# The last norm and the store of a two-block model: from feature-major to token-major output

## The chip, the cores and the metric

The kernel runs on one core of a Trainium2 chip. The metric is the device time of one execution in microseconds (us). Before the change the median of three runs is 906.7 us (905.62, 906.70 and 907.33). One execution was profiled; all rows below are from it.

## The reference, cut to what matters

Two transformer blocks follow each other on 256 tokens of width 1024. The change concerns the very end of the second: the down projection of its MLP, the residual, and the final norm, which divides each token by the root of the mean square over its 1024 features and scales each feature by `g_final`.

```
def rms_norm_2(x, g, eps=1e-5):
    xf = x.astype(float32)
    y = xf * rsqrt(mean(xf * xf, axis=-1, keepdims=True) + eps)
    return y * g
...
    u = rms_norm_2(x, g_mlp) @ w_up          # 256x1024 @ 1024x4096
    x = x + square(relu(u)) @ w_down         # 256x4096 @ 4096x1024
return rms_norm_2(x, g_final)                # 256x1024, float32
```

## The kernel before, in words

**Layout.** Activations are feature-major: a tile has 128 partitions, each a feature, and the 256 tokens (S) lie along the free axis. The width of 1024 is KC = 8 such slices, so xT, the residual stream, is [128, 8, 256]. A sum over features is therefore a sum over partitions and slices, and PE (TensorE) does it with a matmul against the constant tile ones, which holds 1/1024 everywhere: its result has the mean in every one of the 128 partitions.

**Weights.** Class Stream brings a weight tile of 128x1024 by DMA (fetch, line 134, on SyncE's queue, SP), ACT (ScalarE) rounds it to a high part (line 152) and DVE (VectorE) or POOL (GpSimd) subtracts to get the low part (line 158). Function mm3 (lines 358 to 360) then does three matmuls per product: high by high, high by low, low by high.

**Order.** PE's instructions keep the order in which the program writes them; on the other engines and queues a scheduler orders what is ready, and in the part that is looked at here it also keeps the written order.

**The end of the program** (from line 1682). For each of the 8 output slices j, function down does 4 weight tiles of 8 products (96 matmuls) into a PSUM bank. Function residual (line 436, DVE) adds it to xT. Class SumSq squares the slice and adds it up: POOL squares (line 310) and accumulates into ss_acc (line 316) for slices 0 to 6, ACT squares slice 7 into ss_last (line 308). ACT also scales the slice by g_final into og[:, 0, j] (line 1691). The mean needs two matmuls: ones by ss_acc (line 320, put inside the last down, after its second weight tile) and ones by ss_last (line 323, the last thing PE does). Function rsqrt takes Ln and Exp on ACT (line 253), half of that on ACT (line 269), and one Newton step on DVE (lines 271, 272 and 274), all on 128x256. Then line 1696 multiplies og by this row, in three pieces: slices 0 and 1 on DVE, 2 to 4 on DVE, 5 to 7 on POOL, and line 1697 stores each piece, the first and the third by SP, the second by ACT's queue. The host turns the result to token-major. The tile pool tmp, of which rsqrt and SumSq take their tiles, stands in SBUF ahead of the weight buffers (wraw, whi, wlo) and of all pools that are opened later.

Of the kernel before, what the change touches and what calls it, by code (L numbers as in the profile page):

```python
# [8 lines left out]
F32 = mybir.dt.float32  # L9
# [4 lines left out]
ALU = mybir.AluOpType  # L14
# [4 lines left out]
P = 128  # L19
S = 256  # L20
D = 1024
KC = D // P
# [90 lines left out]
class Stream:  # L113
# [53 lines left out]
    def next(self):  # L167
        if not self.ready:
            self.load()
        return self.ready.pop(0)  # L170
# [3 lines left out]
def tile_kernel(ctx: ExitStack, tc: tile.TileContext, a, out: bass.AP):  # L174
    nc = tc.nc
    ctx.enter_context(tc.manual_schedule(engines={mybir.EngineType.PE}))
    V, A, G, PE = nc.vector, nc.scalar, nc.gpsimd, nc.tensor
# [13 lines left out]
    def bank(pool=None, name="bank"):  # L191
        pool = pool or ps_sm
        return pool.tile([P, 512], F32, tag="b", name=name)

    def mmbank():
        return bank(ps_mm, "mmb")
# [19 lines left out]
    def pv(name, j=0, w=1):  # L216
        return par[:, PC[name] + j : PC[name] + j + w]

    def cgv(name):
        return cg[:, CG[name][0] : CG[name][1]]  # L220

    ident = cgv("ident")
# [22 lines left out]
    def lookup(name, *args, **kw):  # L245


        if table["set"] != name:
            load = A.preload_act_table_set(name).ins
            for u in table["users"]:  # L250
                tc.add_manual_dep(load, u.name, NOSYNC, reason="table set")
            table.update(set=name, load=load, users=[])
        ins = A.activation(*args, **kw).ins  # L253
        tc.add_manual_dep(ins, table["load"].name, NOSYNC, reason="table set")
        table["users"].append(ins)
        return ins
# [4 lines left out]
    def rsqrt(mean, eps, n=S, name="rs", pool=None):  # L261

        pool = pool or tmp
        l = tmp.tile([P, n], F32, tag="rs_l", name="rs_l", bufs=1)
        y = tmp.tile([P, n], F32, tag="rs_y", name="rs_y", bufs=1)
        lookup(LNEXP, l, mean, AF.Ln, bias=EPS[eps])
        lookup(LNEXP, y, l, AF.Exp, scale=-0.5)
        yh = l
        A.mul(yh, y, -0.5)
        t = tmp.tile([P, n], F32, tag="rs_t", name="rs_t", bufs=1)  # L270
        V.scalar_tensor_tensor(t, mean, float(eps), y, op0=ALU.add, op1=ALU.mult)
        V.tensor_tensor(t, t, y, op=ALU.mult)
        r = pool.tile([P, n], F32, tag=name, name=name, bufs=2 if name == "rs" else 1)
        V.scalar_tensor_tensor(r, t, -3.0, yh, op0=ALU.add, op1=ALU.mult)
        return r
# [79 lines left out]
    def mm3(dst, hi, lo, x, k, first, last):  # L355

        xh, xl = x[:, k, 0, :], x[:, k, 1, :]
        PE.matmul(dst, lhsT=hi, rhs=xh, start=first, stop=False, skip_group_check=True)  # L358
        PE.matmul(dst, lhsT=hi, rhs=xl, start=False, stop=False, skip_group_check=True)  # L359
        PE.matmul(dst, lhsT=lo, rhs=xh, start=False, stop=last, skip_group_check=True)  # L360

    def g_wide(st, x, b):

        done = 0
        while done < KC:
            k0, nk, hi, lo = st.next()
            for k in range(nk):
                mm3(b[:, :S], hi[:, k, :], lo[:, k, :], x, k0 + k, k0 + k == 0, k0 + k == KC - 1)
                yield
            done = k0 + nk  # L370

    def settle(st, b, n=6):


        if not st.ready:
            st.load()
        hi = st.ready[0][2]
        for _ in range(n):
            PE.matmul(b[:, :S], lhsT=hi[:, 0, :], rhs=hi[:, 0:2, :].rearrange("p k c -> p (k c)"), start=True, stop=True)

    def run(gen):
        for _ in gen:
            pass

    def run_pair(*gens, late=2):

        for g in gens:
            for _ in range(KC - late):
                next(g)
        for g in gens:  # L390
            run(g)

    def down(st, n, x):

        b = mmbank()
        for _ in range(n):
            k0, nk, hi, lo = st.next()
            for k in range(k0, k0 + nk):
                mm3(b[:, :S], hi[:, k - k0, :], lo[:, k - k0, :], x, k, k == 0, k == x.shape[1] - 1)
            yield  # L400
        yield b[:, :S]
# [31 lines left out]
    def residual(j, ps, scale, gain, xnew, ss, mark=None):  # L433

        xj = xT[:, j, :]
        ins = V.scalar_tensor_tensor(xj, ps, float(scale), xj, op0=ALU.mult, op1=ALU.add).ins  # L436
        if mark:
            behind(ins, mark)
        parts = split(xnew, j, xj, gain) if xnew is not None else None
        for s, g in ss:  # L440
            s.add(xj, g)
        return parts
# [37 lines left out]
    ss = SumSq(fast=True)  # L480
# [11 lines left out]
    def hidden(pool, chunks):  # L492

        t = pool.tile([P, chunks * 2 * S + HOME], F32R, name="h")
        return t[:, HOME:].rearrange("p (k i t) -> p k i t", k=chunks, i=2)
# [153 lines left out]
    ss0, ss = ss, SumSq(split=True)  # L649
# [4 lines left out]
    with ExitStack() as rs_ctx:  # L654
# [209 lines left out]
        rstd = rsqrt(ss.mean(), 1e-6)  # L864
# [121 lines left out]
        for t in range(2, 16):  # L986
# [5 lines left out]
                op=ALU.mult,  # L992
# [22 lines left out]
        def columns(tl, w, i):  # L1015

            return n8(tl).rearrange("p n (b i t) -> p n b i t", i=2, t=w)[:, :, :, i, :]

        def per_head(tl):
            return lambda h, n: n8(tl)[own[h], n]  # L1020

        def products(lhsT, rhs):
            b = bank()
            for n in range(8):
                for h, o in enumerate(own):
                    PE.matmul(n8(b)[o, n], lhsT=lhsT(h, n), rhs=n8(rhs)[o, n], start=True, stop=True, skip_group_check=True)  # L1026
                if n % FILL[9] == FILL[9] - 1:
                    fill(FILL[10])
            return b
# [26 lines left out]
        for i, q in enumerate(halves):  # L1056
            b = products(per_head(Y16[i]), T[:, q])
            A.copy(columns(P1[i], 16, 0), columns(b, 16, 0))

        for i, q in enumerate(halves):  # L1060
            b = bank()
# [7 lines left out]
        for i, q in enumerate(halves):  # L1069
            bT = products(per_head(G_[:, q]), P1[i])  # L1070
            bG = products(per_head(P1[i]), G_[:, q])
            for tl, j, b in ((T, 0, bT), (G_, 1, bG)):
                dst = columns(tl[:, q], 16, j)
# [4 lines left out]
        for i, q in enumerate(halves):  # L1078
            b = products(lambda h, n: AA[own[h], h, 2 * i + n // NCH, n % NCH, :], T[:, q])
            A.copy(columns(P2[i], 32, 0), columns(b, 32, 0))  # L1080
        fill(FILL[3])
        for i, q in enumerate(halves):
            b = products(per_head(P2[i]), G_[:, q])
            dst = columns(G_[:, q], 32, 1)
# [3 lines left out]
        def half_bank():  # L1088
            b = bank()
            return b, b[:, :S].rearrange("p (n t) -> p n t", t=CH)  # L1090
# [41 lines left out]
        for c in range(NCH):  # L1132
            cc = slice(c * CH, (c + 1) * CH)
            more = c < NCH - 1
            _, bR = half_bank()
# [12 lines left out]
            _, bSA = half_bank()  # L1148
# [11 lines left out]
            if more:  # L1160
                _, bS = half_bank()
# [106 lines left out]
    ss, ssg = SumSq(split=True), SumSq(split=True)  # L1268
# [21 lines left out]
    with ExitStack() as at_ctx:  # L1290
# [29 lines left out]
        bm = bank()  # L1320
# [231 lines left out]
    with tc.tile_pool(name="ct", bufs=2) as ct:  # L1552
# [63 lines left out]
        rstd = rsqrt(mean_e(), 1e-5)  # L1616
# [44 lines left out]
    with tc.tile_pool(name="h2", bufs=1) as hp, tc.tile_pool(name="ht", bufs=2) as ht:  # L1661
        h = hidden(hp, FC2)
        sd = Stream(nc, wpools, a["dn"], T_DN)
        ahead = [mmbank() for _ in range(3)]
        run_pair(g_wide(st, xf, ahead[0]), g_wide(st, xf, ahead[1]))
        run(g_wide(st, xf, ahead[2]))
        rstd = rsqrt(mean_f(), 1e-5)
        for f_ in range(FC2):
            if f_ < 3:
                b = ahead[f_]  # L1670
            else:
                b = bank() if f_ == 3 else mmbank()
                if f_ == 3:
                    settle(st, b)
                run(g_wide(st, xf, b))
            u = ht.tile([P, S], F32, tag="f_g", name="u")
            V.scalar_tensor_tensor(u, b[:, :S], 0.0, rstd, op0=ALU.max, op1=ALU.mult)
            hf = ht.tile([P, S], F32, tag="f_h", name="hf")
            A.activation(hf, u, AF.Square)
            A.copy(h[:, f_, 0, :], hf)  # L1680
            G.tensor_tensor(h[:, f_, 1, :], hf, h[:, f_, 0, :].bitcast(F32), op=ALU.subtract)  # L1681
        ss = SumSq(split=True)
        bm = bank()
        g_mean = ss.g_mean_into(bm[:, :S], cgv("ones"), True, True)
        og = act.tile([P, 2, KC, S], F32, tag="act", name="og")
        for j in range(KC):
            for i, b in enumerate(down(sd, 4, h)):
                if j == KC - 1 and i == 2:
                    next(g_mean)
            residual(j, b, 1.0, None, None, [(ss, None)])  # L1690
            A.mul(og[:, 0, j, :], xT[:, j, :], pv("g_final_2", j))
        next(g_mean, None)
        rstd = rsqrt(bm[:, :S], 1e-5)
        for j0, j1, eng, q in ((0, 2, V, nc.sync), (2, 5, V, A), (5, 8, G, nc.sync)):
            js = slice(j0, j1)
            eng.tensor_tensor(og[:, 1, js, :], og[:, 0, js, :], rstd[:, None, :].to_broadcast((P, j1 - j0, S)), op=ALU.mult)
            q.dma_start(out[:, js, :], og[:, 1, js, :])

# [135 lines left out]
```

## Time and profile before

| What | Value |
|---|---|
| median of three runs | 906.70 us |
| the profiled execution, time / span | 906.77 us / 904.8 us (the first to the last instruction) |
| PE busy | 882.2 us, 97% of the span |
| DVE / ACT / POOL busy | 609.5 / 511.1 / 353.4 us (67%, 56%, 39%) |
| mean granted TensorE clock | 0.993 of full speed |
| data moved | 154.79 MB, 171 GB/s on average; 1.05 MB of it are the result |

Busy time says how long an engine had something in work. It is an average over stages, so it tells which engine fills most of the span and not what the last microseconds wait for. Times in the timeline are counted from the first instruction; the span of this execution, with two more digits, is 904.85 us, and 1.92 us of the 906.77 lie outside of it.

### The profile page before, as it was taken

How to read it: one execution, taken by the hardware profiler on the slowest of the kernel's cores; microseconds unless marked ns; L12 is line 12 of the kernel's file. 1: busy time of each engine (PE TensorE's matmuls, PEld its weight loads, DVE VectorE, ACT ScalarE, POOL GpSimd, SP SyncE). 2: the span in 40 equal slices, each digit the busy share in tenths (PEclk: the TensorE clock that was granted, in tenths of full speed). 3: DMA queues.
4: the chain of work that ended last, by engine and by line, in shares of the span. 5: the costliest groups of instructions: out<-in, count | busy, mean ns of one | idle time of the engine just before them, and what ended most of it. 6: DMA issues, size and time to landing. Idle time of an engine off the chain costs nothing.

```text
span 904.8 us, 19861 instructions
## 1 busy us (share of the span) xinstructions
PE 882.2 (97%) x7950; PEld 859.8 (95%) x7950; DVE 609.5 (67%) x1010; ACT 511.1 (56%) x904; POOL 353.4 (39%) x381
## 2 busy tenths in 40 slices
PE   8999999999999999999999999999989999999995
PEld 6999999999999899999999999899989999999995
DVE  5666666667989545886665666899866676654452
ACT  6666554448854455756555444666766576654441
POOL 4566652210000456166554788422144133331111
PEclk9999999999999999999999999999999999999998
DMA  6677766673455323567666664544353477666651
GB/s 238 205 221 224 221 213 194 192 219 113 147 144 149 120 83 111 187 177 223 202 191 177 191 193 141 170 121 137 104 177 102 137 214 203 195 198 190 194 179 46
DMA packets 53499, 154.79 MB, mean 171 GB/s; under 512 B 13472, under 2 KB 14880, under 8 KB 53408
## 3 DMA queue, kind: packets, MB, share of 16 engines
q1 hardware_dynamic: 42048, 147.35, 53.6%
q10 hardware_dynamic: 11056, 5.41, 2.1%
q8 instruction: 62, 1.02, 0.4%
q0 software_dynamic: 304, 0.79, 0.3%
q14 instruction: 29, 0.24, 0.1%
HBM read 151.29 MB, written 2.23 MB: 170 GB/s over the span
## 4 chain that ended last, share of the span: by engine, by line
PE 63%; DVE 9%; ACT 2%; issue 2%; DMA 0%; DVEq 0%; POOL 0%; ACTq 0%; SPq 0%
PE mmb L358 16%; PE mmb L360 15%; PE mmb L359 15%; PE bank L359 3%; PE bank L358 3%; PE bank L360 3%; DVE lo L158 2%; PE bank L1026 1%; ACT hi L152 1%; DVE tgg L988 1%; PE bank L688 0%; DVE xT L436 0%; ACT e L253 0%; PE bank L837 0%; PE mmb L569 0%
## 5 line engine op out<-in xcount | busy, mean ns | idle before, releaser
L152 ACT CAST hi<-raw 128x1024 fp32r<-128x1024 f32 (+2 forms) x285 | 292.2, 1027 | 240.6 <-PE mmb L359 162.1
L158 DVE TENSOR_TENSOR lo<-raw,hi 128x1024 fp32r<-128x1024 f32 (+2 forms) x267 | 330.2, 1238 | 143.1 <-ACT hi L152 141.6
L358 PE MATMUL mmb<-h,hi 128*128 128x256 f32 x608 | 168.1, 277 | 0.0
L359 PE MATMUL mmb<-h,hi 128*128 128x256 f32 x608 | 167.8, 276 | 0.0
L360 PE MATMUL mmb<-h,lo 128*128 128x256 f32 x608 | 167.8, 276 | 0.0
L358 PEld LDWEIGHTS mmb<-h,hi 128*128 128x128 f32 x608 | 114.1, 188 | 0.0
L359 PEld LDWEIGHTS mmb<-h,hi 128*128 128x128 f32 x608 | 114.1, 188 | 0.0
L360 PEld LDWEIGHTS mmb<-h,lo 128*128 128x128 f32 x608 | 114.1, 188 | 0.0
L158 POOL TENSOR_TENSOR lo<-raw,hi 128x256 fp32r<-128x256 f32 x72 | 54.6, 790 | 86.1 <-ACT hi L152 85.2
L509 POOL TENSOR_TENSOR f_s<-f_s,rs 128x256 f32<-128x256 f32 x44 | 56.3, 1281 | 61.5 <-ACT f_s L253 61.5
L513 POOL TENSOR_TENSOR h<-f_h,h 128x256 fp32r<-128x256 f32 x44 | 59.0, 1342 | 31.8 <-ACT h L512 30.0
L358 PE MATMUL mmb<-xf,hi 128*128 128x256 f32 x248 | 68.4, 276 | 0.0
L359 PE MATMUL mmb<-xf,hi 128*128 128x256 f32 x248 | 68.4, 276 | 0.0
L360 PE MATMUL mmb<-xf,lo 128*128 128x256 f32 x248 | 68.4, 276 | 0.0
L1681 POOL TENSOR_TENSOR h<-hf,h 128x256 fp32r<-128x256 f32 x32 | 32.1, 1007 | 69.2 <-ACT h L1680 43.9
L358 PE MATMUL mmb<-xa,hi 128*128 128x256 f32 x176 | 50.2, 285 | 1.7 <-ACT hi L152 1.7
L316 POOL TENSOR_TENSOR ss_acc<-ss_acc,ss_sq 128x256 f32<-128x256 f32 x38 | 45.9, 1207 | 10.7 <-ACT ss_sq L308 8.3
L360 PE MATMUL mmb<-xa,lo 128*128 128x256 f32 x176 | 49.3, 280 | 0.2 <-DVE lo L158 0.2
L359 PE MATMUL mmb<-xa,hi 128*128 128x256 f32 x176 | 49.2, 280 | 0.0
L358 PE MATMUL bank<-xa,hi 128*128 128x256 f32 x176 | 48.9, 278 | 0.0
L360 PE MATMUL bank<-xa,lo 128*128 128x256 f32 x176 | 48.7, 277 | 0.0
L360 PE MATMUL mmb<-xc,lo 128*128 128x256 f32 x176 | 48.7, 276 | 0.0
(418 smaller groups left out, 2701.5 us busy)
## 6 DMA issues: line engine op xcount, KB each, us to landing
raw<-in_g SPq DMA_DIRECT2D x43, 512.0 KB, 4.4
raw<-in_u SPq DMA_DIRECT2D x43, 512.0 KB, 4.3
raw<-in_d SPq DMA_DIRECT2D x32, 512.0 KB, 3.6
raw<-in_up SPq DMA_DIRECT2D x32, 512.0 KB, 4.3
raw<-in_dn SPq DMA_DIRECT2D x32, 512.0 KB, 4.3
raw<-in_win SPq DMA_DIRECT2D x29, 512.0 KB, 4.0
raw<-in_ckv SPq DMA_DIRECT2D x16, 512.0 KB, 4.0
raw<-in_wout SPq DMA_DIRECT2D x16, 512.0 KB, 3.6
```

What stands on the lines that cost most here:

```text
L152: cast = nc.scalar.copy(hi[:, :n], raw[:, :n]).ins
L158: self.last = eng.tensor_tensor(lo[:, q], raw[:, q], hi[:, q].bitcast(F32), op=ALU.subtract).ins
L316: G.tensor_tensor(self.acc, self.acc, dst, op=ALU.add)
L358: PE.matmul(dst, lhsT=hi, rhs=xh, start=first, stop=False, skip_group_check=True)
L359: PE.matmul(dst, lhsT=hi, rhs=xl, start=False, stop=False, skip_group_check=True)
L360: PE.matmul(dst, lhsT=lo, rhs=xh, start=False, stop=last, skip_group_check=True)
L509: marks["pool"] = G.tensor_tensor(sl, sl, rstd, op=ALU.mult).ins
L513: G.tensor_tensor(h[:, f, 1, :], hf, h[:, f, 0, :].bitcast(F32), op=ALU.subtract)
L988: V.tensor_tensor(prv, TU[:, 0:t, 0:t].rearrange("p s j -> p j s"), AU[:, 0:t, t][:, None, :].to_broadcast((P, t, t)), op=ALU.mult,)
L1026: PE.matmul(n8(b)[o, n], lhsT=lhsT(h, n), rhs=n8(rhs)[o, n], start=True, stop=True, skip_group_check=True)
L1681: G.tensor_tensor(h[:, f_, 1, :], hf, h[:, f_, 0, :].bitcast(F32), op=ALU.subtract)
```

## The change: what it does, and the diff

The result leaves token-major: out is now [128, 2, 1024], with a token on each partition and two groups (t) of 128 tokens. PE turns og, the slices that are scaled by g_final: function turn does two transposes (128x128, against the identity) per slice into four PSUM banks, `turned[t][j // 4]`. The mean is now wanted per token on the partitions: four matmuls with the squares as the stationary operand and one column of ones, into two columns of a PSUM bank. rsqrt works on 128x2. ACT (for t = 0) and DVE (for t = 1) multiply the turned banks by the token's number, from PSUM into SBUF, in four pieces of 128x512, and four stores of 256 KB follow, three by SP and one by ACT's queue. POOL has no part in the scaling any more.

```
-        bm = bank()
-        g_mean = ss.g_mean_into(bm[:, :S], cgv("ones"), True, True)
         og = act.tile([P, 2, KC, S], F32, tag="act", name="og")
         for j in range(KC):
-            for i, b in enumerate(down(sd, 4, h)):
-                if j == KC - 1 and i == 2:
-                    next(g_mean)
+            for b in down(sd, 4, h):
+                pass
             residual(j, b, 1.0, None, None, [(ss, None)])
             A.mul(og[:, 0, j, :], xT[:, j, :], pv("g_final_2", j))
-        next(g_mean, None)
-        rstd = rsqrt(bm[:, :S], 1e-5)
-        for j0, j1, eng, q in ((0, 2, V, nc.sync), (2, 5, V, A), (5, 8, G, nc.sync)):
-            js = slice(j0, j1)
-            eng.tensor_tensor(og[:, 1, js, :], og[:, 0, js, :], rstd[:, None, :].to_broadcast((P, j1 - j0, S)), op=ALU.mult)
-            q.dma_start(out[:, js, :], og[:, 1, js, :])
+        turned = [[bank() for _ in range(2)] for _ in range(2)]
+        bm = mmbank()
+
+        def turn(j):
+            for t in range(2):
+                PE.transpose(turned[t][j // 4][:, j % 4 * P : (j % 4 + 1) * P], og[:, 0, j, t * P : (t + 1) * P], ident)
+
+        for j in range(KC - 1):
+            turn(j)
+        for t in range(2):
+            for i, sq in enumerate((ss.acc, ss.last)):
+                PE.matmul(bm[:, t : t + 1], lhsT=sq[:, t * P : (t + 1) * P], rhs=cgv("ones")[:, 0:1], start=i == 0, stop=i == 1, skip_group_check=True)
+        turn(KC - 1)
+        rstd = rsqrt(bm[:, 0:2], 1e-5, n=2, name="rs_t2")
+        res = og[:, 1].rearrange("p (t j) s -> p t (j s)", t=2)
+        for i in range(2):
+            for t in range(2):
+                dst = res[:, t, i * 512 : (i + 1) * 512]
+                if t:
+                    V.tensor_scalar(dst, turned[t][i], rstd[:, t : t + 1], None, op0=ALU.mult)
+                else:
+                    A.mul(dst, turned[t][i], rstd[:, t : t + 1])
+                (A if i and not t else nc.sync).dma_start(out[:, t, i * 512 : (i + 1) * 512], dst)
...
-    out = nc.dram_tensor("out_0", (P, KC, S), F32, kind="ExternalOutput").ap()
+    out = nc.dram_tensor("out_0", (P, S // P, D), F32, kind="ExternalOutput").ap()
...
-    return np.ascontiguousarray(o.transpose(1, 0, 2).reshape(D, S).T)[None]
+    return np.ascontiguousarray(o.transpose(1, 0, 2).reshape(S, D))[None]
```

How PE's order changes. Before, in the middle of the last slice's down, between its second and third weight tile (mmb is the PSUM bank of the slice, bank that of the mean, cg the tile of constants with ones and the identity):

```order
L358 MATMUL mmb<-h,hi 128x256
L359 MATMUL mmb<-h,hi 128x256
L360 MATMUL mmb<-h,lo 128x256
L320 MATMUL bank<-ss_acc,cg 128x256
L358 MATMUL mmb<-h,hi 128x256
```

After, the 96 matmuls of the slice stand together, and this is the end of PE's program, behind them (x14: so many in a row):

```order
L360 MATMUL mmb<-h,lo 128x256
L1696 MATMUL bank<-cg,og 128x128 x14
L1702 MATMUL mmb<-cg,ss_acc 128x1
L1702 MATMUL mmb<-cg,ss_last 128x1
L1702 MATMUL mmb<-cg,ss_acc 128x1
L1702 MATMUL mmb<-cg,ss_last 128x1
L1696 MATMUL bank<-cg,og 128x128 x2
```

So the half of the mean that stood inside the tile has moved behind it, and 14 of the 16 transposes stand between the last down matmul and the mean. On DVE, behind the last residual, the difference is this (rs_t is the helper tile of the Newton step, rs_t_12107 its result rs_t2):

```order
-L271 SCALAR_TENSOR_TENSOR rs_t<-bank,rs_y 128x256
-L272 TENSOR_TENSOR rs_t<-rs_t,rs_y 128x256
-L274 SCALAR_TENSOR_TENSOR rs<-rs_t,rs_l 128x256
-L1696 TENSOR_TENSOR og<-og,rs 128x512
-L1696 TENSOR_TENSOR og<-og,rs 128x768
-L1831 UNCONDITIONAL_BRANCH
+L271 SCALAR_TENSOR_TENSOR rs_t<-mmb,rs_y 128x2
+L272 TENSOR_TENSOR rs_t<-rs_t,rs_y 128x2
+L274 SCALAR_TENSOR_TENSOR rs_t_12107<-rs_t,rs_l 128x2
+L1710 TENSOR_SCALAR og<-bank,rs_t_12107 128x512 x2
```

The number and order of DVE's steps stay, but they read and write two columns instead of 256, and the scaling reads PSUM.

## Rows read from the trace of the kernel before

**Rows 1.** The page, part 4: the chain that ended last, by engine.

```profile
PE 63%; DVE 9%; ACT 2%; issue 2%; DMA 0%; DVEq 0%; POOL 0%; ACTq 0%; SPq 0%
```

**Rows 2.** Timeline, last down tile: start us, us, engine, line, operation, out<-in, count.

```profile
883.44 0.50 ACT L1691 ACTIVATE og<-xT,par 128x256 f32<-128x256 f32 x1
...
890.44 0.28 PE L360 MATMUL mmb<-h,lo 128*128 128x256 f32 x1
...
890.56 0.59 PE L320 MATMUL bank<-ss_acc,cg 128*128 128x256 f32 x2
...
891.11 0.28 PE L359 MATMUL mmb<-h,hi 128*128 128x256 f32 x1
...
893.62 0.28 PE L360 MATMUL mmb<-h,lo 128*128 128x256 f32 x1
```

**Rows 3.** Timeline, the tail; in brackets the idle time before and its releaser.

```profile
894.40 0.42 ACT L308 ACTIVATE ss_last<-xT 128x256 f32<-128x256 f32 x1 [10.45 <-DVE xT L436]
...
894.86 0.70 PE L323 MATMUL bank<-ss_last,cg 128*128 128x256 f32 x2 [0.96 <-ACT ss_last L308]
895.60 0.47 ACT L253 ACTIVATE rs_l<-bank,epsc 128x256 f32<-128x256 f32 x1 [0.39 <-PE bank L323]
...
898.00 3.17 DVE L1696 TENSOR_TENSOR og<-og,rs 128x512 f32<-128x512 f32 x2
898.05 2.31 POOL L1696 TENSOR_TENSOR og<-og,rs 128x768 f32<-128x768 f32 x1 [12.66 <-DVE rs L274]
898.72 2.00 SPq L1697 DMA_DIRECT2D out<-og  x2
901.20 0.35 ACTq L1697 DMA_DIRECT2D out<-og  x1
```

**Rows 4.** DMA view of 898 to 905 us: rate by slice, then stores with us to landing.

```profile
GB/s 0 0 0 0 0 0 0 0 12 386 410 386 293 12 0 0 0 0 228 456 386 456 386 439 369 456 386 456 369 106 0 0 0 0 0 0 0 0 0 0
...
out<-og ACTq DMA_DIRECT2D x1, 384.0 KB, 2.6
out<-og SPq DMA_DIRECT2D x1, 256.0 KB, 2.1
```

**Rows 5.** PE groups by line and form: count, busy us, mean ns, idle before.

```profile
L1600 PE MATMUL bank<-cg,ce 128*128 128x128 f32 x16 | 2.4, 272 | 0.0
...
L555 PE MATMUL bank<-one,rs_m 1*128 1x1 f32 x4 | 0.6, 250 | 0.0
```

**Rows 6.** The same view for ACT and DVE: small operations, and operations from PSUM.

```profile
L253 ACT ACTIVATE el<-bank 128x2 f32<-128x2 f32 x1 | 0.2, 163 | 0.0
...
L597 ACT ACTIVATE Vm<-mmb,rmN 128x256 f32<-128x256 f32 x8 | 3.7, 470 | 3.1 <-DVE tgg L994 2.1 <-PE mmb L571 1.0
...
L1065 ACT COPY tgg<-bank 128x512 f32<-128x512 f32 x1 | 0.6, 586 | 0.9 <-PE bank L1064 0.9
...
L1390 DVE SCALAR_TENSOR_TENSOR m<-mx,par 128x4 f32<-128x4 f32 x4 | 1.2, 290 | 0.0
...
L1397 DVE TENSOR_TENSOR den<-den,es 128x4 f32<-128x4 f32 x4 | 0.7, 184 | 2.8 <-ACT e L253 2.8
...
L1065 DVE COPY tgg<-bank 128x512 f32<-128x512 f32 x1 | 0.7, 691 | 3.8 <-PE bank L1064 3.8
```

**Rows 7.** Stretches A:B: width; PE, PEld, DVE, ACT, POOL busy (x); clock; DMA share; GB/s.

```profile
898.50:899.50 1.00, 0.00 (x0) 0.00 (x0) 1.00 (x2) 0.00 (x0) 1.00 (x1) 0.86 0.00 0
899.50:904.80 5.30, 0.00 (x0) 0.00 (x0) 1.67 (x1) 0.00 (x0) 0.85 (x1) 0.50 0.50 198
```

**Rows 8.** The down weights on SP: landing time (page, part 6), and four issues (timeline).

```profile
raw<-in_dn SPq DMA_DIRECT2D x32, 512.0 KB, 4.3
...
868.54 8.49 SPq L134 DMA_DIRECT2D raw<-in_dn  x4
```

**Rows 9.** Line 358's matmuls on h and on mg: duration ns least/median/most, first and last start.

```profile
L358 PE MATMUL mmb<-h,hi x608: 276/276/469, 132.1 to 893.4; 128*128 128x256 f32 x152
...
L358 PE MATMUL mmb<-mg,hi x64: 276/281/471, 289.1 to 343.3; 128*128 128x256 f32 x64
```

## Prediction

> **What bounds the kernel now.** I read the chain of work that ended last first: 63% of the span is TensorE (PE) matmul, nearly all of it in lines 358 to 360 [rows 1]. The change touches none of those matmuls; all its edits lie behind the last one. So the stretch to read is the tail, by the timeline, from the last down matmul to the end of the span at 904.85 us.
>
> In that timeline the tail is one chain with nothing beside it. The last down matmul starts at 893.62 [rows 2]. Then [rows 3]: the residual on VectorE (DVE), the last square on ScalarE (ACT) at 894.40, the mean on PE at 894.86, Ln on ACT at 895.60, Exp, and three DVE steps of a 256-wide Newton step, done when line 1696 starts at 898.00. So rsqrt costs 895.60 to 898.00, **2.40 us**. Then the scaling: DVE does two pieces in 3.17 us while GpSimd (POOL) does one in 2.31 us. The three stores are issued at 898.72, about 900.37 and 901.20. The traffic view cuts 898 to 905 into 40 slices of 0.175 us [rows 4]: the first store moves between 899.4 and 900.5, then the engines stand idle until 901.15, then the other two run back to back to about 903.2. The span ends 1.65 us after the last byte. From the first issue to the end it takes 6.13 us, though 1.05 MB at the 410 GB/s of the full slices is only 2.56 us.
>
> **The change part by part.** I place the tail of the changed kernel on the clock of the profiled execution.
>
> *The early half of the mean goes from inside the last down tile.* Line 359 starts at 891.11, where without line 320 it would have started two intervals of 0.11 after 890.44, at 890.66 [rows 2]. Removed: 0.44 us. Weights are no limit there: ACT works in order, and the tile's last cast stands ahead of the og slice that it scaled at 883.44. So everything up to the last square moves up 0.44: last down matmul 893.18, last square done at 894.40 + 0.42 - 0.44 = 894.38.
>
> *PE transposes instead.* Fourteen stand in PE's order between the last down matmul and the new mean, and they need only og slices 0 to 6, which are there long before. Sixteen of this form, in four groups of four, kept PE busy for 2.4 us, 0.60 a group, and one lasts 0.272 [rows 5], so they start (0.60 - 0.27)/3 = 0.11 apart, and 14 take 1.54: from 893.29 to 894.83. This lies partly under the residual and the square (they end at 894.38), so 0.45 us of it is on the path.
>
> *The mean per token.* Four matmuls of one column. The nearest row, the 1-column matmuls of line 555, shows two records per fp32 call: four records for two calls, 0.6 us in all with 0.25 for one, so 0.117 apart [rows 5]. Eight passes: 894.83 + 7 x 0.117 + 0.25 = 895.90, and with the 0.04 from PE to ACT that the old mean shows (0.70 from 894.86, Ln at 895.60) Ln starts at **895.94, 0.34 later than before**. Bounds: if passes came 0.05 apart, 0.5 earlier; if each lasted its 0.25 in full, 0.9 later. I take 0.117, the only row of one column. The two transposes of the last slice come behind this, ready by 896.2; their bank is read second, so they cost nothing.
>
> *rsqrt on two columns instead of 256.* An ACT operation on two columns takes 0.163, DVE operations on four take 0.184 to 0.290 [rows 6]; the gap to the next is about 0.04, as between the mean and Ln. Two on ACT, at 0.18 each: 0.44. Three on DVE, at 0.18 each, the low row, since POOL is idle here and the rows stand in busier stages: 0.66. Sum 1.10 instead of 2.40: r is there at **897.04**. Bounds 0.95 and 1.5. The halving on ACT lies beside DVE's first steps, as before.
>
> *Scaling from PSUM.* ACT and DVE take two 128x512 pieces each and POOL none. An ACT copy of 128x512 from PSUM takes 0.586, a 128x256 scaled per partition 0.470, so one piece lies between 0.586 and twice 0.470; I take 0.70, near the copy, because most of the fixed part is paid once. On DVE the copy takes 0.691. First issue at 897.04 + 0.70 + 0.04 = **897.78** (898.72 before), the second on SP about 0.35 behind (what one issue occupies its queue), the last two near 898.5 (901.20 before). The old 3.17 us on DVE and 2.31 on POOL are gone.
>
> *The store.* The same 1.05 MB, now in four pieces of 256 KB, all issued within 0.8 us, so that the pause of 0.7 us in the traffic closes. First data 0.85 after the first issue (the old first store: 898.72 to about 899.5), 2.56 us of data at 410 GB/s (386 to 456 in the full slices: 2.72 to 2.30), 1.65 to the end: 897.78 + 0.85 + 2.56 + 1.65 = **902.84, against 904.85: 2.0 us less.**
>
> The Trainium skill (DMA: Bandwidth & Descriptors, Anatomy of one DMA) speaks against four small stores: some 2.0 us fixed for each, plus bytes over 436 GB/s. By that the last byte would be confirmed 2.0 + 2.4 us after the first issue, at 902.2, and with the 1.05 us that the trace shows from the last landing (901.20 + 2.6 = 903.8) to the end the kernel would gain 1.6 instead of 2.0. The trace has 2.1 us for a whole 256 KB store [rows 4] where that formula estimates 2.6, so I keep to the trace.
>
> The sum stands against the profiled execution, 906.77 us (span 904.85 and 1.92 around it); that is 0.07 above the median of 906.70. Forecast: **904.7**. With all small costs at their upper ends (0.4 on rsqrt, 0.24 on ACT, 0.16 on data, 0.3 on PE) the gain is 0.9; with all at their lower ends (0.15, 0.11, 0.26, 0.2) it is 2.7. The three runs of before lie 1.7 us apart, so medians add half a microsecond either way: 903.6 to 906.2 for this case.
>
> **The rivals.**
>
> *PE becomes the bound of the tail.* If transposes and one-column passes do not overlap and each takes its whole duration, they cost 14 x 0.272 + 8 x 0.25 = 5.8 instead of 2.6, and the time is 904.7 + 3.2 = 907.9. Against it: in the rows they do overlap, four in 0.60. Half of that overlap lost gives 906.3.
>
> *PE runs the tail at its lower clock.* The granted clock still averages 0.86 from 898.5 to 899.5 and is 0.50 after, that is 2.4 and 1.2 GHz [rows 7], so it falls some five microseconds after the dense matmuls. If the tail ran at the lower level, 14 x 0.11 and 8 x 0.117 would double: up to 2.5 more, 907.2. Against it: PE's new work ends at 896.2, well before the fall. The Trainium skill (TensorE: Matmul & The Clock Gate, Part 4) says that transposes do not count as busy; by that rule the fall would come a little earlier, and the trace of before, which has no transposes at a tail, cannot show it.
>
> *SP serves its stores one at a time.* Three of the four stores go through SP. If each had to land (2.1 us) before the next moved, the last lands at 897.78 + 6.3 = 904.1 and the span ends 1.05 later: 907.1 in all. For it: the two SP stores of before never overlapped. Against it: the down weights, 512 KB each on the same queue, take 4.3 us to land, and four were issued within 8.49 us, 2.7 apart [rows 8], so SP overlaps transfers.
>
> *The layout moves, and the matmuls get slower.* The new small tile rs_t2 in the pool tmp takes 32 bytes of each partition, and every pool opened after tmp (raw, hi, lo, the hidden h and all of the mixing tiles) starts 32 bytes higher; in the built programs the first raw buffer goes from byte 87,872 to 87,904. Matmuls of one and the same size have two durations in the trace: a median of 276 ns on h, of 281 on mg [rows 9]. If operand addresses decide which, the 1,824 matmuls on h alone (three times 608) could cost 5 ns x 1,824 = 9.1 us more: 913.8. It decides as soon as 400 matmuls change over, since 400 x 5 ns eat the 2.0 us. Against it: the matmuls on mg show both durations, at least 276 and 281 in the median, with the same buffers, which looks like the stage and not the address. It could as well go the other way and give some microseconds.
>
> *The change does less than it says*, if DVE's two old pieces are slow by themselves and not for POOL beside them. That costs nothing here: the new pieces are others, from PSUM.
>
> **How the numbers follow.** About 0.2%, 1.8 us, is what a measurement of this kernel can tell from no change, so faster means below 904.9, which is only just above my forecast. The forecast's case has 0.70: 0.48 of it under 904.9 and 0.22 above. PE as the bound 0.07, the lower clock 0.03, SP one at a time 0.07: all within 0.2%. Layout 0.13: 0.09 slower, 0.04 faster. Sum: faster 0.52, same 0.39, slower 0.09. The range reaches from 903.3 to 906.5: it takes in the forecast's case and the half-way forms of the PE and SP rivals, and leaves out the layout and the full price of the others, less than 0.2 together.
>
> **What would show it.** Right: line 320 gone from the last tile and the last down matmul about 893.2; 14 transposes 0.11 apart right behind it; Ln near 895.9; from Ln to the first scaling about 1.1 us; scaling 0.7 each; four stores issued between 897.8 and 898.6; full traffic for 2.5 us without a pause; all else unchanged up to 893. Wrong: Ln after 897 (PE or its clock), a pause between the SP stores, or a time up to the last down matmul that differs by more than one microsecond from before (layout).

## The result, and the profile after

The changed kernel takes **921.8 us** (median of 4 runs, 920.09 to 923.12) where the kernel before, run beside it, takes 907.0: a ratio of 1.0153, 95% interval 1.0129 to 1.0178. Forecast were 904.7 us, and 903.3 to 906.5 as the range. The kernel became slower by some 15 us through a change that rewrites the last 11.

These lines of its page answer to [rows 1] and to the table of before: the span, PE's busy time, the chain, and one of the costliest groups.

```profile
span 921.4 us, 19904 instructions
...
PE 905.1 (98%) x7970; PEld 883.1 (96%) x7970; DVE 607.6 (66%) x1010; ACT 511.0 (55%) x906; POOL 354.1 (38%) x380
...
PE 68%; DVE 5%; ACT 2%; issue 2%; DMA 1%; ACTq 0%; DVEq 0%; POOL 0%; SPq 0%
...
L358 PE MATMUL mmb<-h,hi 128*128 128x256 f32 x608 | 170.1, 280 | 0.0
```

PE is busy 22.9 us longer (882.2 before) with only 20 more instructions, none of them long; ACT, DVE and POOL do what they did. So the time is in matmuls that nobody touched. PE's idle time fell from 22.6 to 16.3 us in exchange, which is why the span grew by 16.6 and not by 22.9.

**The tail is as forecast.** The timeline of the changed kernel from the last down matmul on, which answers to [rows 2, 3]:

```profile
911.81 0.28 PE L360 MATMUL mmb<-h,lo 128*128 128x256 f32 x1
...
911.93 1.69 PE L1696 MATMUL bank<-cg,og 128*128 128x128 f32 x14
912.59 0.42 ACT L308 ACTIVATE ss_last<-xT 128x256 f32<-128x256 f32 x1 [10.43 <-DVE xT L436]
...
913.46 0.28 PE L1702 MATMUL mmb<-cg,ss_acc 128*128 128x1 f32 x2
...
914.05 0.36 PE L1702 MATMUL mmb<-cg,ss_last 128*128 128x1 f32 x2
...
914.45 0.26 ACT L253 ACTIVATE rs_l<-mmb,epsc 128x2 f32<-128x2 f32 x1 [1.04 <-PE mmb L1702]
914.74 0.20 ACT L253 ACTIVATE rs_y<-rs_l 128x2 f32<-128x2 f32 x1
...
914.98 0.16 DVE L271 SCALAR_TENSOR_TENSOR rs_t<-mmb,rs_y 128x2 f32<-128x2 f32 x1 [2.42 <-ACT rs_y L253]
...
915.63 1.27 ACT L1712 ACTIVATE og<-bank,rs_t 128x512 f32<-128x512 f32 x2 [0.45 <-DVE rs_t L274]
915.63 1.41 DVE L1710 TENSOR_SCALAR og<-bank,rs_t 128x512 f32<-128x512 f32 x2
916.34 1.33 SPq L1713 DMA_DIRECT2D out<-og  x3
916.93 0.35 ACTq L1713 DMA_DIRECT2D out<-og  x1
```

And the stores in the DMA view, 915 to 921.5 us in 40 slices (before: [rows 4]), with the issues, KB each and us to landing:

```profile
GB/s 0 0 0 0 0 0 0 0 0 0 0 0 0 151 403 378 391 416 403 403 416 391 416 403 416 391 416 403 416 240 0 0 0 0 0 0 0 0 0 0
...
out<-og SPq DMA_DIRECT2D x3, 256.0 KB, 2.4
out<-og ACTq DMA_DIRECT2D x1, 256.0 KB, 2.8
```

The transposes follow the last matmul without a gap, rsqrt takes 914.45 to 915.63, both engines scale at once, and the pause in the stores is gone. From the start of the last down matmul to the end of the span it is 921.4 - 911.8 = 9.6 us; before it was 904.85 - 893.62 = 11.2.

**The loss lies before it, a little everywhere.** The tile view gives for one line and tile: count, least/median/most duration in ns, first and last start. Before (for h see [rows 9]):

```profile
L358 PE MATMUL bank<-xa,hi x176: 276/276/469, 13.4 to 131.8; 128*128 128x256 f32 x176
...
L358 PE MATMUL mmb<-xc,hi x176: 276/276/281, 369.6 to 487.7; 128*128 128x256 f32 x176
L358 PE MATMUL bank<-xc,hi x176: 276/276/281, 371.7 to 490.4; 128*128 128x256 f32 x176
...
L358 PE MATMUL mmb<-xf,hi x248: 276/276/276, 717.4 to 805.9; 128*128 128x256 f32 x124
```

After (xa and xc are what the first and second FFN read, xf what the MLP reads; h is the hidden tile of all three):

```profile
L358 PE MATMUL bank<-xa,hi x176: 277/280/469, 11.9 to 134.7; 128*128 128x256 f32 x176
...
L358 PE MATMUL mmb<-xc,hi x176: 277/280/283, 376.4 to 498.4; 128*128 128x256 f32 x176
L358 PE MATMUL bank<-xc,hi x176: 277/280/283, 378.5 to 501.2; 128*128 128x256 f32 x176
...
L358 PE MATMUL mmb<-xf,hi x248: 277/280/283, 730.1 to 821.1; 128*128 128x256 f32 x124
...
L358 PE MATMUL mmb<-h,hi x608: 276/281/384, 135.0 to 911.6; 128*128 128x256 f32 x152
```

The lag grows: where xa's line begins, the changed kernel is 1.5 us ahead (11.9 against 13.4), at its end 2.9 behind (134.7 against 131.8), then 6.8 when xc begins, 10.8 at its end, 12.7 when xf begins, 18.2 at the last down matmul (911.6 against 893.4 [rows 9]). No stall explains that, only a slower pace, as the matmuls counted in fixed stretches show. Columns: stretch, its length, PE busy (count), granted clock, DMA share, GB/s. Before, in xa, in h of the first FFN and in xc:

```profile
20.00:130.00 110.00, 110.00 (x969) 1.00 0.69 212
140.00:195.00 55.00, 54.76 (x483) 1.00 0.62 187
390.00:490.00 100.00, 100.00 (x885) 1.00 0.66 196
```

After, in the same stretches, and in h of the second FFN:

```profile
20.00:130.00 110.00, 110.00 (x938) 1.00 0.67 208
140.00:195.00 55.00, 55.00 (x470) 1.00 0.61 183
390.00:490.00 100.00, 100.00 (x855) 1.00 0.63 191
510.00:560.00 50.00, 50.00 (x444) 1.00 0.61 188
```

Where PE is never idle, the length of a stretch by the count is the distance from one start to the next (a short stretch counts those at its edges too, so only stretches of equal length compare): 110.00/969 = 113.5 ns before, 110.00/938 = 117.3 after; 113.4 and 117.0 in h; 113.0 and 117.0 in xc. In xa and xc PE is never idle in either kernel, in h for 0.24 us of 55 before, and the granted clock is 1.00 (the 2.4 GHz level) in both, so it is neither a wait nor the clock. I call the two paces **close** (113) and **wide** (117). Some 4 ns on the 2,880 matmuls of xa, xc and xf and on the 1,296 of h in the first FFN and the MLP are 16.7 us; smaller groups, whose matmuls became slower too, come on top. In h of the second FFN the changed kernel runs close (50.00/444 = 112.6).

### The profile page after: what moved, and what is told of

Its sections match the earlier page's. It is cut to its first block, busy times and chain, and to the rows that moved or that the text cites. A ratio compares the mean times of both kernels' runs of the same rounds, so it can differ in the third digit from the quotient of the medians.

```text
span 921.4 us, 19904 instructions
## 1 busy us (share of the span) xinstructions
PE 905.1 (98%) x7970; PEld 883.1 (96%) x7970; DVE 607.6 (66%) x1010; ACT 511.0 (55%) x906; POOL 354.1 (38%) x380
## 4 chain that ended last, share of the span: by engine, by line
PE 68%; DVE 5%; ACT 2%; issue 2%; DMA 1%; ACTq 0%; DVEq 0%; POOL 0%; SPq 0%
PE mmb L358 17%; PE mmb L359 17%; PE mmb L360 17%; PE bank L359 3%; PE bank L358 3%; PE bank L360 3%; DVE lo L158 1%; PE bank L1026 1%; ACT hi L152 1%; DVE tgg L988 0%; PE bank L837 0%; PE bank L1349 0%; PE bank L688 0%; ACT e L253 0%; PE bank L1376 0%
## 5 line engine op out<-in xcount | busy, mean ns | idle before, releaser
L358 PE MATMUL mmb<-h,hi 128*128 128x256 f32 x608 | 170.1, 280 | 0.0
L359 PE MATMUL mmb<-h,hi 128*128 128x256 f32 x608 | 170.0, 280 | 0.0
L360 PE MATMUL mmb<-h,lo 128*128 128x256 f32 x608 | 170.0, 280 | 0.0
L360 PEld LDWEIGHTS mmb<-h,lo 128*128 128x128 f32 x608 | 116.0, 191 | 0.0
L509 POOL TENSOR_TENSOR f_s<-f_s,rs 128x256 f32<-128x256 f32 x44 | 56.9, 1296 | 66.4 <-ACT f_s L253 66.4
L359 PE MATMUL mmb<-xf,hi 128*128 128x256 f32 x248 | 69.4, 280 | 0.0
L358 PE MATMUL mmb<-xf,hi 128*128 128x256 f32 x248 | 69.4, 280 | 0.0
L316 POOL TENSOR_TENSOR ss_acc<-ss_acc,ss_sq 128x256 f32<-128x256 f32 x38 | 48.1, 1266 | 10.8 <-ACT ss_sq L308 8.4
L359 PE MATMUL mmb<-xc,hi 128*128 128x256 f32 x176 | 49.2, 280 | 0.0
```

The lines of the kernel that those rows point to most:

```text
L316: G.tensor_tensor(self.acc, self.acc, dst, op=ALU.add)
L509: marks["pool"] = G.tensor_tensor(sl, sl, rstd, op=ALU.mult).ins
```

## The experiments

My theory is the layout: rs_t2 moves everything opened after the pool tmp by 32 bytes, x stays, and that alone sets the pace. Its main rival is that PE's changed program or the new tail does it. The table says how many bytes further on than in the kernel before the buffers lie in each kernel that ran (per partition, in the built program), with the times and the pace that the tile and window views show for x (xa, xc and xf) and h. The ratios are to runs of the kernel before beside each kernel, on the same chip, whose medians lie between 906.9 and 908.5.

| Kernel | x | raw, hi | lo | h and later | median us | ratio, 95% interval | x | h |
|---|---|---|---|---|---|---|---|---|
| before | 0 | 0 | 0 | 0 | 907.0 | | close | close |
| changed | 0 | 32 | 32 | 32 | 921.8 | 1.0153 (1.0129 to 1.0178) | wide | wide, second FFN close |
| e1 | 0 | 0 | 0 | 0 | 905.7 | 0.9971 (0.9956 to 0.9987) | close | close |
| e2 | 0 | 32 | 32 | 32 | 924.4 | 1.0169 (1.0132 to 1.0206) | wide | close in the profiled run |
| e3 | 0 | 64 | 64 | 64 | 922.9 | 1.0164 (1.0130 to 1.0198) | wide | close |
| e4 | 0 | 0 | 0 | 32 | 917.2 | 1.0095 (1.0065 to 1.0124) | close | wide |
| e6 | 32 | 32 | 32 | 32 | 907.0 | 1.0015 (0.9976 to 1.0054) | close | close |
| e7 | 0 | 0 | 32 | 32 | 930.4 | 1.0246 (1.0208 to 1.0283) | wide | wide |
| e10 | 0 | 128 | 128 | 128 | 926.8 | 1.0207 (1.0167 to 1.0247) | wide | wide, MLP close |
| e11 | 0 | 0 | 0 | 0 | 916.8 | 1.0105 (1.0058 to 1.0151) | wide | wide, second FFN close |
| e12 | 0 | 32 | 32 | 32 | 929.5 | 1.0259 (1.0243 to 1.0274) | wide | wide, second FFN close |
| e13 | 32 | 32 | 32 | 32 | 904.4 | 0.9974 (0.9957 to 0.9991) | close | close |

### e1: the new tail without the shift

```
-        rstd = rsqrt(bm[:, 0:2], 1e-5, n=2, name="rs_t2")
+        rstd = rsqrt(bm[:, 0:2], 1e-5, n=2, name="rhoN")
```

> The changed kernel, whose one new tile for the last norm's two columns takes the place of the earlier tile rhoN instead of a place of its own, so that no buffer lies 32 bytes further on than in the kernel before; every instruction stays in its order. Layout theory: the 18 us were lost by the shift, and the tail gained its forecast 2.0 us, so about 904.7 us (903.5 to 905.5), with the x and h matmuls back at 276 ns in the lines of L358 to L360. Rival, that the changed tail or PE's changed program costs the time: about 921.8 us, matmuls at 280 ns.

Measured 905.66, 0.29% under the kernel before beside it (907.64), with x and h close; in xa:

```profile
20.00:130.00 110.00, 110.00 (x971) 1.00 0.66 211
```

All of the changed program, and none of the loss.

### e2: the shift without the new tail

```
-        r = tmp.tile([P, 2], F32, tag=name, name=name, bufs=1)
+        r = tmp.tile([P, 10 if name == "rmN" else 2], F32, tag=name, name=name, bufs=1)[:, :2]
```

> The kernel before with nothing changed but one small tile made 32 bytes wider, so that all pools opened after it lie 32 bytes further on, as in the changed kernel. Layout theory: about 923.7 us (921.8 plus the tail's 2.0), matmuls at 280 ns. Rival (changed tail or program): 907.0 us, matmuls at 276 ns.

Measured 924.4: the loss without the change. With e1 this settles which part of the change costs. One thing did not fit: the four runs reach from 918.89 to 926.47, and the profiled one is the lowest. In it, x is wide and h close (columns as above):

```profile
20.00:130.00 110.00, 110.00 (x928) 1.00 0.65 206
140.00:195.00 55.00, 55.00 (x488) 1.00 0.59 191
```

h of the first FFN lies here at the same addresses as in the changed kernel, which ran it wide. Addresses alone do not decide, then.

### e3: 64 bytes

The changed kernel with the edit of e2 as well.

> The changed kernel with the same tile 32 bytes wider, so that everything behind it lies 64 bytes further on than in the kernel before. If the place within 64 bytes decides: about 904.7 us. If any shift against the buffers that stay in place decides: about 921.8 us or another slow value, above 915. Rival (changed tail or program): 921.8 us.

Measured 922.93: no rule of 64 bytes for x. But h, which moves together with the weights, is close (tile view of xa and h):

```profile
L358 PE MATMUL bank<-xa,hi x176: 279/281/468, 13.6 to 137.0; 128*128 128x256 f32 x176
...
L358 PE MATMUL mmb<-h,hi x608: 276/276/384, 137.3 to 911.0; 128*128 128x256 f32 x152
```

That pointed at distances between buffers.

### e4: h and later alone

```
     wlo = ctx.enter_context(tc.tile_pool(name="wlo", bufs=4))
+    ctx.enter_context(tc.tile_pool(name="pad1", bufs=1)).tile([P, 8], F32, name="pad1")
```

> The kernel before with 32 unused bytes behind the weight buffers: the weights stay where they were, and h and the pools of the mixing stages lie 32 bytes further on. If the place of the weights decides: 907.0 us. If the place of the activations (h and the mixing tiles) decides: slow in those stages, h at 280 ns, x at 276 where x did not move; worked out from 4.4 ns on some 2,000 h matmuls about 915 us. Rival (changed tail or program): 907.0 us.

Measured 917.15. Only the tile that was moved against the weights is wide; the two stretches of x count the same as before:

```profile
20.00:130.00 110.00, 110.00 (x969) 1.00 0.68 211
140.00:195.00 55.00, 55.00 (x467) 1.00 0.59 180
390.00:490.00 100.00, 100.00 (x885) 1.00 0.64 198
```

55.00/467 is 117.8 ns: 4.4 more than before, and on 1,824 matmuls 8.0 of the 9.5 us lost.

### e6: everything together

```
+    ctx.enter_context(tc.tile_pool(name="pad0", bufs=1)).tile([P, 8], F32, name="pad0")
     act = ctx.enter_context(tc.tile_pool(name="act", bufs=3))
```

> The kernel before with 32 unused bytes ahead of the activation buffers, so that x, the weights, h and the mixing tiles all lie 32 bytes further on and keep their distances to one another. If the distance between the moving operand and the weights decides: 907.0 us, the x and h matmuls close together as in the kernel before. If the place of each by itself decides: slow, 915 to 924 us. The third theory, that any new layout is slower than this one: also 915 to 924 us.

Measured 907.04, no difference that the runs can tell. In xa and in h of the first FFN:

```profile
20.00:130.00 110.00, 110.00 (x969) 1.00 0.71 212
140.00:195.00 55.00, 54.76 (x484) 1.00 0.64 189
```

Every buffer of the wide kernel e2 has the same address here, except x and helper tiles of tmp, and x is close again. So it is the distance between moving operand and weights, not the place of either, and not that any other layout is worse. Of its ten runs eight lie between 905.6 and 910.1 and two at 918.2 and 918.8; those two were not profiled, and why they differ is open.

### e7: lo without hi

```
+    ctx.enter_context(tc.tile_pool(name="pad1", bufs=1)).tile([P, 8], F32, name="pad1")
     wlo = ctx.enter_context(tc.tile_pool(name="wlo", bufs=4))
```

> The kernel before with 32 unused bytes between the buffers of hi and of lo: x, raw and hi stay, lo and h and everything later lie 32 bytes further on. If the distance of moving operand and weights decides: h against hi is moved, so h is slow as when h alone was moved (917.2 us); x against hi is not, against lo it is, so of x a third to a half slow, together 917 to 924 us. If the place of hi alone decides for x: x fast, 917 us. If the place of each buffer by itself decides nothing more than chance: any time between 907 and 924.

Measured 930.38, more than any theory had said. In xa and in h:

```profile
20.00:130.00 110.00, 110.00 (x934) 1.00 0.68 206
140.00:195.00 55.00, 55.00 (x465) 1.00 0.60 182
```

x is as slow as if hi had moved too. So one moved partner is enough to make the whole sequence wide, the two matmuls against hi included: hi by xh, hi by xl and lo by xh take turns on PE, and the pace is that of the round. One thing this run does not separate: lo has moved against hi as well as against x, and either could be what makes x wide here. The "third to a half" that I expected for x was wrong.

### e10: 128 bytes

As e2, with 34 in place of 10.

> The kernel before with the small tile 128 bytes wider: weights, h and later 128 bytes further on, x in place. If the distance of x to the weights decides within 32 or 64 bytes: 907.0 us; within 128 bytes, the same, but 64 bytes gave 922.9 already with the changed kernel, so within 128 only; if it decides within 256 bytes or more: slow in x, fast in h, 917 to 924 us.

Measured 926.81. x wide again; h, expected close, was so only in the MLP. The close distances are rare among those tried: for x the one of the kernel before, and none of 32, 64 or 128 more. Shifts of 256 bytes and over were not tried, for want of room in SBUF. But the kernel before already holds many distances: its three x buffers lie 16,384 bytes apart in the built program, the four buffers of hi and of lo 4,352, the slices that PE reads in them 512 to 2,048. All of these are multiples of 256, and xa, xc and xf are all close. So it looks as if the pattern repeated every 256 bytes or oftener; no run shifted a buffer by 256 to test it.

### e11: no settle

Function settle (line 372, its matmuls on line 379) issues six matmuls of hi by hi, after which the x matmuls go on. It is called at three places. The kernel leaves these 18 out; their results are overwritten in any case.

```
-        for _ in range(n):
+        for _ in range(0):
             PE.matmul(b[:, :S], lhsT=hi[:, 0, :], rhs=hi[:, 0:2, :].rearrange("p k c -> p (k c)"), start=True, stop=True)
```

> The kernel before without the six matmuls by which each call of settle (18 in all) goes ahead of a stage; nothing else is left out, and their results are overwritten. If these matmuls bring PE into the close spacing: most x and h matmuls stay at the wide spacing, 4 ns on some 5,500 matmuls, about 920 us or more. If the layout decides by itself: 907.0 us less up to 2 us for the matmuls left out.

Measured 916.8, although the layout is that of before, 18 matmuls fewer. The profiled run is the slowest of the four (921.74; the others 915.22 to 917.57), so it may have more wide stretches than they. In xa, in h of the first FFN, in xc and in h of the second FFN:

```profile
20.00:130.00 110.00, 110.00 (x935) 1.00 0.67 207
140.00:195.00 55.00, 55.00 (x470) 1.00 0.60 183
390.00:490.00 100.00, 100.00 (x851) 1.00 0.64 191
510.00:560.00 50.00, 50.00 (x443) 1.00 0.61 184
```

The trace of the kernel before holds the switch itself, inside xa. Ahead of the first settle x is wide, behind it close, with the same buffers. First the kernel before, and then e11 in the last of these stretches, where it has stayed wide:

```profile
14.50:24.50 10.00, 10.00 (x87) 1.00 0.59 176
...
25.11 1.06 PE L379 MATMUL bank<-hi 128*128 128x256 f32 x6
...
28.00:38.00 10.00, 10.00 (x91) 1.00 0.64 181
...
28.00:38.00 10.00, 10.00 (x88) 1.00 0.57 170
```

Neither theory alone: the right distance does not bring the close pace by itself. PE has to come into it, and at this place the six matmuls bring it; the next x matmul starts 0.89 us behind the first of them (26.00). e1 and e13 show that it can also come without: between 15.2 and 24.8 us, ahead of the first settle, PE does 87 matmuls in them and 84 in the kernel before. And in e11 the second FFN's h is close without any settle.

### e12: more settling in the shifted layout

`def settle(st, b, n=24)` in the changed kernel.

> The changed kernel, in its shifted layout, with 24 instead of 6 matmuls in each of the three calls of settle (54 more of 0.113 to 0.118 us, 6.1 to 6.4 us). If the shifted layout only makes it less likely that PE goes over to the close spacing at a settle, and more tries bring it there: 921.8 + 6.3 - 18 = about 910 us. If the shifted layout does not allow the close spacing for x at all: 921.8 + 6.3 = about 928 us, x at 117 to 118 ns from start to start.

Measured 929.52, as expected if the layout forbids it. In xa:

```profile
20.00:130.00 110.00, 110.00 (x937) 1.00 0.66 202
```

At this wrong distance 24 of these matmuls bring no more than six; at the right one six were enough.

### e13: the tile ahead of x, a version that beats both

```
-        rstd = rsqrt(bm[:, 0:2], 1e-5, n=2, name="rs_t2")
+        rstd = rsqrt(bm[:, 0:2], 1e-5, n=2, name="rs_t2", pool=cons)
```

> The changed kernel with the new tile of the last norm taken from the pool of constants, ahead of the activations: x, weights, h and the mixing tiles all lie 32 bytes further on than in the kernel before, with their distances as they were. If the distances decide: 904.7 us (903.3 to 906.5, the forecast for the change). If a place of its own for the tile, or the changed program, costs the time: 921.8 us.

Measured 904.43, against 906.90 beside it: 0.9974 (0.9957 to 0.9991). It is the changed kernel with one argument added. Its page and its tile view of xc and h:

```profile
PE 882.4 (98%) x7970; PEld 860.3 (95%) x7970; DVE 607.6 (67%) x1010; ACT 511.2 (57%) x906; POOL 352.0 (39%) x380
```

```profile
L358 PE MATMUL mmb<-xc,hi x176: 276/276/276, 368.4 to 486.7; 128*128 128x256 f32 x176
...
L358 PE MATMUL mmb<-h,hi x608: 276/276/386, 131.8 to 892.5; 128*128 128x256 f32 x152
```

The same 7,970 instructions that kept PE busy for 905.1 us in the changed kernel take 882.4 here.

## Why the prediction was wrong, and where it was right

**What failed is the weight given to the rival on the layout.** It named the tile, the 32 bytes and the pools that move, and gave it 0.09 on the slower side. The step that failed is the reason against it: "the matmuls on mg show both durations, at least 276 and 281 in the median, with the same buffers, which looks like the stage and not the address." The row was right and the conclusion was not. Two conditions have to meet: the distance must allow the close pace (e4, e6, e13), and PE must have come into it (e11). A tile that shows both durations at one place shows that the second condition exists; it says nothing against the first. The prediction's own sign of the layout, a time up to the last down matmul that differs by more than one microsecond, came out at 18.

A better reading was open: that x and h sit at 276 in the median while the kernel takes care to settle PE is a sign of a pace that can be lost, and the trace of before shows both paces within xa, on the same buffers (e11). The kernel's own code pointed at places, too: class Stream starts a weight tile 32 elements (128 bytes) further on in its buffer where that tile is to be the moving operand (line 149).

**Its price was too small as well.** The term was 5 ns on the 1,824 matmuls on h alone, 9.1 us. e4, which moves h alone, lost 9.5 us, 8.0 of it on these matmuls, so that term was good. But h moved together with its weights, which in e3 left it close; what moved against the weights was x, and its 2,880 matmuls were not in the sum. In the changed kernel they are some 11.5 us at 4 ns each. The point from which it decides, 400 matmuls, was passed tenfold.

**The change itself was costed right**, shown by e1 and e13: 2.0 and 2.5 us under the kernel before beside them, where 2.0 were forecast (the intervals of the two reach from 0.8 to 4.0), and e13's median of 904.4 stands against 904.7. Step by step, counted from the start of the last down matmul (forecast 893.18, measured 911.81 in the changed kernel):

| Step | Forecast | Measured |
|---|---|---|
| transposes begin | +0.11 | +0.12 |
| one-column passes begin | +1.65 | +1.65 |
| Ln | +2.76 | +2.64 |
| scaling begins | +3.86 | +3.82 |
| first store issued | +4.60 | +4.53 |
| end of the span | +9.66 | +9.6 |

- *PE transposes, and mean per token.* 14 transposes 0.11 apart hold. The eight passes begin 913.46 and the last pair starts at 914.05; that is 0.10 from pass to pass where 0.117 were taken, and Ln follows 0.12 earlier than forecast. So PE did not become the bound of the tail. Nor did it run at its lower clock: PE is done at 914.7, and the granted clock is 1.00 up to 918.
- *rsqrt on two columns* took 1.18 (914.45 to 915.63) for 1.10, which takes back most of what Ln gained: ACT's operations were 0.26 and 0.20 for 0.18, DVE's 0.16.
- *Scaling from PSUM*: two pieces in 1.27 on ACT and 1.41 on DVE, 0.64 and 0.70 each for 0.70.
- *The store*: from the first issue to the end 5.06 were forecast, and 921.4 - 916.34 = 5.06 measured; full traffic from 917.3 to 919.7 without a pause. So SP did not serve its stores one at a time. The Trainium skill (DMA: Bandwidth & Descriptors, Anatomy of one DMA) gives its formula for DMAs that GpSimd issues; these stores are issued by SP and ACT. By it the last landing was estimated 4.4 after the first issue, which with the 1.05 of the trace behind it made 5.45; the rows of before were nearer.

**What is shown and what is not.** Shown: 32 bytes of layout cost the whole loss and some (e1, e2); the distance of moving operand to weights decides whether x and h can run close (e4, e6, e13); what PE did before decides in addition (e11), and more settling did not help at a wrong distance (e12). Not shown: what PE does in the wide pace. That the read of the moving operand and the load of the next weights get in each other's way would fit; no run measured it, and the recorded load times do not tell, since on xc their median is 188 ns before and after. The Trainium skill (TensorE: Matmul & The Clock Gate, Part 2, Step-by-step) says that weights come by a read port of their own, so that loading the next tile's weights takes no read bandwidth from the running matmul. If nothing else tied the two operands together, e4 and e6 would have taken the same time; they are 10 us apart, so something does, and whether it is read bandwidth stays open. Open too is why h at a right distance runs wide in some stages or runs (the first FFN and the MLP of the changed kernel) and close in others.

## What to carry to other kernels

A new tile is a change of layout: look up which buffers it moves, and against which other operands, before you cost anything else; where PE is the bound, 4 ns on thousands of matmuls outweigh anything that a tail can give. Put a small new tile into a place that already exists, or ahead of all operands of PE, so that the distances stay. If a kernel becomes slower where it was not changed, count PE's instructions in equal stretches before and after: the same busy share with fewer instructions, at the same granted clock, is a change of pace and no wait.

## What the runs showed of the hardware that was not expected

- Back-to-back pairs of a 128x128 weight load and a 256-column matmul (fp32r) run at two paces at a granted clock of 1.00 (the 2.4 GHz level): about 113 and 117 ns from start to start, with records of 276 and 280 to 281 ns.
- Which one depends on how far the moving operand lies from the weights in a partition. For x, weights 32, 64 and 128 bytes further on gave the wide pace (924.4, 922.9 and 926.8 us); moving both by 32 bytes changed nothing (907.04 us).
- It depends on what PE did before, too: 18 matmuls fewer, in three places, cost 8.3 us (e11: 916.80 against 908.49), and in the kernel before the pace changes at such a place with no buffer moved (87 matmuls in 10 us ahead of it, 91 behind).
- Moving lo and h by 32 bytes, with hi and x in place, was the dearest of all: 930.4 us, with x and h both wide.
